# A two-layer encoder trunk on one core: four column blocks together in the FFN's first product, one block of x turned on TensorE, HBM reads issued later

## Chip, cores and metric

The kernel runs on one core of a Trainium2 chip. The metric is the device time of one execution in microseconds (us), the median of several executions of the same program.

## The reference

The reference is a pre-norm transformer encoder in 32-bit floats: 256 tokens of width D = 2048, two layers. The even layer mixes by retention and neighbourhood attention, the odd one by differential attention; each layer then has cross-attention into 256 memory tokens and a SwiGLU feed-forward network (FFN) with 5632 hidden columns. What stands around the change is this:

```python
def rms_norm(x, g):
    xf = x.astype(jnp.float32)
    y = xf * lax.rsqrt(jnp.mean(xf * xf, axis=-1, keepdims=True) + RMS_EPS)
    return (y * g.astype(jnp.float32)).astype(x.dtype)

def swiglu_ffn(h, w_in, w_out):
    g, u = jnp.split(h @ w_in, 2, axis=-1)
    return (jax.nn.silu(g) * u) @ w_out

# in each layer i, after the mixer:
    m = rms_norm(mem, norm_mem_g[i])
    x = x + memory_cross_attention(rms_norm(x, norm_xattn_g[i]), m, w_xq[i], w_xkv[i], w_xo[i], xq_g[i], xk_g[i])
    x = x + swiglu_ffn(rms_norm(x, norm_ffn_g[i]), w_ffn_in[i], w_ffn_out[i])
```

## The kernel before

**Layout.** x stays in SBUF as `x_sb`, the 256 tokens as two halves of 128 on the partitions, the 2048 columns as four blocks of 512. A product needs its left operand with the columns on the partitions, so x has to be turned before each of them. A product's left operand is kept as a pair of fp32r tiles, a rounded high part and a low part (`hTfh` and `hTfl` for the FFN, `hTxh` and `hTxl` for the cross-attention, `hTh` and `hTl` for the next layer's mixer), and so is each weight (`wh`, `wl`). Every product is the sum of three: high by `wh` (L313), high by `wl` (L314), low by `wh` (L315).

**Weights.** A weight piece of 512 rows by 512 columns (1 MB) is read by the SP queue into `raw`. `prepare()` makes from each half of it `wh` by a copy on ScalarE (L287) and `wl` by a subtraction on VectorE (L288), up to three units ahead of their use (`LOOK`). A *unit* is one such half, 256 rows by 512 columns: two row tiles, two token halves and three products make 12 matmuls of 128x512. `gemm()` runs the units of one weight matrix; the lists in `plan` set their order. By default a column block takes all its units before the next block begins. `woven(n, nu, early)` lets the first two column blocks take their first units, then the rest, then the blocks that are left: with 8 units, block 0 takes units 0 to 5, block 1 units 0 to 5, then 6 and 7 of each. Each column block holds two accumulators (`acc`, one per token half) in PSUM, out of a pool with two buffers of each.

**The FFN.** It runs in three groups of 4, 4 and 3 hidden blocks. In the first product (`w_ffn_in`) a hidden block is two column blocks, gate and up. All units with rows 0 to 511 need the left operand made of block 0 of x, those with rows 512 to 1023 need block 1, and so on.

**Turning x.** In the product before (`w_xo`, a single row piece, so two units to a block) the epilogue adds a finished block to x on VectorE (L722) and starts a *feed* of it. `regroup()` transposes 32x32 squares on VectorE into `zz` (L381, one instruction per token half), writes `zz` to a DRAM buffer `zd` on the SP queue (L383) and reads it back with the squares regrouped by four DMAs of the POOL queue (L385). The rest of the feed multiplies by the gain: ScalarE writes the high part (L400, four instructions), VectorE the low part (L402, eight). SP's queue also issues the weight reads, in its order.

**What sets the order.** Feeds and the attention's steps are generators held by a `Side` object. `gemm` takes one step of them after each unit (two where `steps=2`); a step waits for the count of units that the generator yielded, `MOVE = 5` between a feed's reads and its gain. A `gate` drains a feed before the unit that needs it. A scheduler then orders the instructions of each engine, so the queues are shown below as they stand in the built program.

## Time and profile before

| | before |
|---|---|
| three executions | 2489.2, 2491.04, 2495.09 us |
| median | 2491.04 us |
| profiled execution | 2492.25 us |
| its span, first to last instruction | 2490.3 us |
| granted TensorE clock, mean over the span | 0.998 |
| busy: TensorE / its weight loads / VectorE / ScalarE / GpSimd | 99 / 82 / 59 / 48 / 6 % |
| read from HBM | 487.93 MB, with the writes 206 GB/s over the span |

The span is measured on the profiled execution, and 1.95 us of that execution lie outside it. PE is TensorE, PEld its weight loads, DVE VectorE, ACT ScalarE, POOL GpSimd, SPq the queue of DMA issues on SyncE. In a row of a timeline stand the start in us, the duration, the engine, the line, the operation, what is written and from what, the shapes and the count; a bracket gives the engine's idle time just before and what ended it. "acc<-wh,hTfh" is a matmul into acc out of these two operands, hTfh the stationary one and wh the moving one with its 512 columns; "x8" is eight instructions told as one row.

### The profile page before, as it was taken

To read this page: it belongs to the slowest core of one execution; us is meant where nothing else is said; L and a number is where in the kernel's file an instruction comes from. 1 tells how busy PE (TensorE), PEld (TensorE's weight loads), DVE (VectorE), ACT (ScalarE), POOL (GpSimd) and SP (SyncE) were. 2 spreads that over 40 slices of the span, in tenths; PEclk is the share of its full clock that TensorE was granted. 3 is DMA by queue.
4 is the path that set the end of the run, shared out by engine and by line. 5 is a ranking of instruction groups with operands and counts; after the bars stand their busy time and mean duration, and the time that the engine had idled before them with its cause. 6 is when DMAs were issued, how large, how long until landed. Compare 5 with 4: busy or idle time off the path is not lost.

```text
span 2490.3 us, 28635 instructions
## 1 busy us (share of the span) xinstructions
PE 2459.9 (99%) x11168; PEld 2038.3 (82%) x11168; DVE 1480.4 (59%) x1845; ACT 1188.5 (48%) x1538; POOL 144.4 (6%) x223
## 2 busy tenths in 40 slices
PE   8999999999999999999999999999999999999999
PEld 6888888878888888888878888888788888888887
DVE  6775565775555555545567766766655545555554
ACT  5554464555443444444455555655544444443443
POOL 1000001110000000000010000010100000000000
PEclk9999999999999999999999999999999999999999
DMA  8545567566675666656675544674766556665665
GB/s 288 180 163 182 181 229 237 202 218 205 204 234 187 214 208 218 204 190 233 223 233 169 169 169 164 214 251 166 236 223 217 203 200 205 230 209 192 213 213 175
DMA packets 250856, 513.92 MB, mean 206 GB/s; under 512 B 11488, under 2 KB 12128, under 8 KB 250720
## 3 DMA queue, kind: packets, MB, share of 16 engines
q1 hardware_dynamic: 239856, 485.52, 57.1%
q0 software_dynamic: 8704, 24.13, 4.2%
q10 hardware_dynamic: 2160, 2.44, 0.3%
q8 instruction: 87, 1.43, 0.2%
q14 instruction: 49, 0.40, 0.0%
HBM read 487.93 MB, written 24.12 MB: 206 GB/s over the span
## 4 chain that ended last, share of the span: by engine, by line
PE 94%; DMA 3%; DVE 2%; issue 0%; ACT 0%; POOL 0%; ACTq 0%; POOLq 0%; DVEq 0%
PE acc L313 30%; PE acc L314 30%; PE acc L315 30%; DMA zd<-zz 1%; DMA zz<-zd 1%; PE pt L337 1%; DVE wl L288 1%; DMA raw<-in_w_in_ab 1%; DVE x_sb L722 0%; PE pt L526 0%; PE pa_s L418 0%; PE pa_s L417 0%; PE pa_s L416 0%; PE pa_r L576 0%; DVE zz L381 0%
## 5 line engine op out<-in xcount | busy, mean ns | idle before, releaser
L288 DVE TENSOR_TENSOR wl<-raw,wh 128x1024 fp32r<-128x1024 f32 (+1 forms) x865 | 1054.4, 1221 | 881.6 <-ACT wh L287 881.3
L287 ACT CAST wh<-raw 128x1024 fp32r<-128x1024 f32 (+1 forms) x865 | 909.6, 1052 | 1177.8 <-PE acc L315 1153.1
L313 PE MATMUL acc<-wh,hTfh 128*128 128x512 f32 x1408 | 550.8, 391 | 11.8 <-ACT hTfh L400 11.8
L314 PE MATMUL acc<-wl,hTfh 128*128 128x512 f32 x1408 | 549.7, 390 | 0.0
L315 PE MATMUL acc<-wh,hTfl 128*128 128x512 f32 x1408 | 548.6, 390 | 0.0
L313 PE MATMUL acc<-wh,hTh 128*128 128x512 f32 x832 | 331.8, 399 | 9.6 <-ACT wh L287 8.1
L314 PE MATMUL acc<-wl,hTh 128*128 128x512 f32 x832 | 325.6, 391 | 0.9 <-DVE wl L288 0.9
L315 PE MATMUL acc<-wh,hTl 128*128 128x512 f32 x832 | 325.5, 391 | 0.0
L313 PEld LDWEIGHTS acc<-wh,hTfh 128*128 128x128 f32 x1408 | 265.4, 189 | 69.2 <-ACT hTfh L400 14.3
L315 PEld LDWEIGHTS acc<-wh,hTfl 128*128 128x128 f32 x1408 | 265.4, 189 | 56.1 <-DVE hTfl L402 0.7
L314 PEld LDWEIGHTS acc<-wl,hTfh 128*128 128x128 f32 x1408 | 265.6, 189 | 55.1
L314 PE MATMUL acc<-wl,aTh 128*128 128x512 f32 x704 | 274.0, 389 | 2.9 <-DVE wl L288 2.9
L315 PE MATMUL acc<-wh,aTl 128*128 128x512 f32 x704 | 273.9, 389 | 0.0
L313 PE MATMUL acc<-wh,aTh 128*128 128x512 f32 x704 | 273.9, 389 | 0.0
L313 PEld LDWEIGHTS acc<-wh,hTh 128*128 128x128 f32 x832 | 156.9, 189 | 39.8 <-ACT wh L287 8.1
L315 PEld LDWEIGHTS acc<-wh,hTl 128*128 128x128 f32 x832 | 156.6, 188 | 33.9
L314 PEld LDWEIGHTS acc<-wl,hTh 128*128 128x128 f32 x832 | 157.0, 189 | 31.7 <-DVE wl L288 2.3
L385 POOL DMA_DIRECT2D zz<-zd x168 | 91.7, 553 | 1553.7 <-DMA zd<-zz 1450.3
L314 PEld LDWEIGHTS acc<-wl,aTh 128*128 128x128 f32 x704 | 132.1, 188 | 30.7 <-DVE wl L288 3.4
L313 PEld LDWEIGHTS acc<-wh,aTh 128*128 128x128 f32 x704 | 132.1, 188 | 27.5
L315 PEld LDWEIGHTS acc<-wh,aTl 128*128 128x128 f32 x704 | 132.1, 188 | 27.4
L313 PE MATMUL acc<-wh,oTh 128*128 128x512 f32 x256 | 100.2, 392 | 0.0
(185 smaller groups left out, 1939.7 us busy)
## 6 DMA issues: line engine op xcount, KB each, us to landing
raw<-in_w_ffn_in SPq DMA_DIRECT2D x176, 1024.0 KB, 4.9
raw<-in_w_ffn_out SPq DMA_DIRECT2D x88, 1024.0 KB, 5.1
raw<-in_w_in_ab SPq DMA_DIRECT2D x55, 1024.0 KB, 5.1
raw<-in_w_in_c SPq DMA_DIRECT2D x48, 1024.0 KB, 5.1
zd<-zz SPq DMA_DIRECT2D x42, 512.0 KB, 3.7
zz<-zd POOLq DMA_DIRECT2D x168, 128.0 KB, 4.9
raw<-in_w_out_ab SPq DMA_DIRECT2D x16, 1024.0 KB, 5.1
raw<-in_w_xkv SPq DMA_DIRECT2D x16, 1024.0 KB, 5.0
```

The lines of the kernel that those rows point to most:

```text
L287: nc.scalar.copy(wh[:, js], raw[:, rs])
L288: nc.vector.tensor_sub(wl[:, js], raw[:, rs], wh[:, js])
L313: nc.tensor.matmul(acc[t], lhsT=hi[:, kt, ts], rhs=wh[:, j], start=first and j == 0, stop=False)
L314: nc.tensor.matmul(acc[t], lhsT=hi[:, kt, ts], rhs=wl[:, j], start=False, stop=False)
L315: nc.tensor.matmul(acc[t], lhsT=lo[:, kt, ts], rhs=wh[:, j], start=False, stop=last and j == 1)
L337: nc.tensor.transpose(pt[:, j, t * P:(t + 1) * P], srcs[t][:, c:c + P], ident)
L385: nc.gpsimd.dma_start(zT[32 * j:32 * j + 32].rearrange("a (i n) -> a i n", i=4), zd[:, :, j].rearrange("i a n -> a i n"))
```

## The change

Three things change in the code.

- **Order of the first FFN product.** In the first group, `by_rows(n, 4)` takes the place of `woven(n, 8, 6)`: the first four column blocks take rows 0 to 511 together (two units each), then rows 512 to 1023, and so on; the other four follow one by one. Four blocks need eight accumulators. The third pair takes buffers of the pool `ps_t` and the fourth of `ps_a` (`wide`), which the attention uses at other times.
- **Block 0 of x turned on TensorE.** Between `w_xo` and the FFN, block 0 no longer goes through DRAM: `feed_turns`, as two tasks of one half each, turns it with TensorE transposes into PSUM (`turn`, four to a task) and writes the gain's high and low parts from there (`gained`). Blocks 1 to 3 go as before.
- **Reads issued later.** `regroup` becomes a generator with a step of `LAND = 2` units between the SP write and the four POOL reads, and one of `MOVE - LAND` after them. The sums of squares of a feed come ahead of it. This holds for all feeds and for the turning of the FFN's activations (`act_T`).

```diff
--- before.py
+++ after.py
@@ -24,7 +24,7 @@
 SCALE = HD ** -0.5
 LAM_INIT = 0.8 - 0.6 * math.exp(-0.3 * 1)
 NEG = -1e30
-MOVE = 5
+LAND, MOVE = 2, 5
 FFN_GROUPS = ((0, 4), (4, 8), (8, 11))
 
 OPENING = {2: (2, 3), 4: (-1,), 6: (4, 5), 8: (-2,), 10: (6, 7), 12: (-3,), 14: (-4,)}
@@ -226,6 +226,11 @@
         head += [(b, u) for b in range(lead) for u in range(early, nu)]
         return head + [(b, u) for b in range(lead, nblocks) for u in range(nu)]
 
+    def by_rows(nblocks, lead):
+
+        head = [(b, 2 * c + u) for c in range(4) for b in range(lead) for u in range(2)]
+        return head + [(b, u) for b in range(lead, nblocks) for u in range(8)]
+
 
     plan = []
 
@@ -254,7 +259,7 @@
         for g0, g1 in FFN_GROUPS:
             n = 2 * (g1 - g0)
             cols = [c + b * NB for b in range(g0, g1) for c in (0, HID)]
-            phase(w_ffn_in[layer], K4, cols, woven(n, 8, 6) if g0 == 0 else None)
+            phase(w_ffn_in[layer], K4, cols, by_rows(n, 4) if g0 == 0 else None)
             phase(w_ffn_out[layer], tuple(b * NB for b in range(g0, g1)), four, woven(4, n, n - 2))
     units = [(i, b, u) for i, ph in enumerate(plan) for b, u in ph[3]]
     ahead = deque()
@@ -289,7 +294,7 @@
         ahead.append((wh, wl))
         at["unit"] += 1
 
-    def gemm(kts, src, epi, gate=None, steps=1):
+    def gemm(kts, src, epi, gate=None, steps=1, wide=False):
         hi, lo = src
         w2, rows, cols, order = plan[at["phase"]]
         at["phase"] += 1
@@ -298,7 +303,10 @@
         for b, u in order:
             side.drain((gate or {}).get(u, ()))
             if b not in accs:
-                accs[b] = [ps_acc.tile([P, NB], F32, tag=f"acc{t}", name=f"acc{t}") for t in range(2)]
+                pools = ((ps_acc, f"acc{t}") for t in range(2))
+                if wide and b in (2, 3):
+                    pools = ((ps_t, "pt"), (ps_t, "pt")) if b == 2 else ((ps_a, "pa"), (ps_a, "pa"))
+                accs[b] = [q.tile([P, NB], F32, tag=tag, name=f"acc{t}") for t, (q, tag) in enumerate(pools)]
                 left[b] = nu
             while len(ahead) <= LOOK and at["unit"] < len(units):
                 prepare()
@@ -381,18 +389,29 @@
             nc.vector.transpose(zt[:, :, :, t], srcs[t].rearrange("p (k j a) -> p j k a", j=4, a=32))
         zd = dram.tile([4, 32, 4, T], F32, name="zd")
         nc.sync.dma_start(zd.rearrange("i a j n -> (i a) (j n)"), zt.rearrange("p j k t b -> p (j k t b)"))
+        yield LAND
         for j in range(4):
             nc.gpsimd.dma_start(zT[32 * j:32 * j + 32].rearrange("a (i n) -> a i n", i=4),
                                 zd[:, :, j].rearrange("i a n -> a i n"))
+        yield MOVE - LAND
         return zT.rearrange("p (i k t b) -> p i k t b", i=4, k=4, t=2)
 
+    def feed_turns(dst, b, u, srcs, gi, layer, ssr):
+
+        pt = turn(srcs, u)
+        for j in range(2):
+            k = 4 * b + 2 * u + j
+            gained(dst, k, pt[:, j], gain(gi, layer, k))
+        square_sum(ssr[0][:, u, b:b + 1], srcs[u])
+        return
+        yield
+
     def feed(dst, b, srcs, gi, layer, ssr, room):
-        zT = regroup(srcs, room)
         for t in range(2):
             square_sum(ssr[0][:, t, b:b + 1], srcs[t])
         if b == 3:
             finish_rstd(ssr)
-        yield MOVE
+        zT = yield from regroup(srcs, room)
         for k in range(4):
             g = gain(gi, layer, 4 * b + k)
             hi, lo = (x[:, 4 * b + k].rearrange("p (t i b) -> p t i b", t=2, i=4) for x in dst)
@@ -800,14 +819,16 @@
 
         def epi_xo(b, acc):
             add_x(acc, b)
-            tasks.extend(feed_x(hT, b, 3, layer, ssr, ("", "", "qT", "kT")[b]))
+            if b == 0:
+                tasks.extend(side.add(feed_turns(hT, b, u, x_block(b), 3, layer, ssr), u) for u in range(2))
+            else:
+                tasks.extend(feed_x(hT, b, 3, layer, ssr, ("", "", "qT", "kT")[b]))
 
         gemm((0,), xo, epi_xo, gate={0: heads[:2], 1: heads[2:]}, steps=2)
         gate = by_unit(tasks)
 
         def act_T(aT, zs, kt):
-            zT = regroup(zs)
-            yield MOVE
+            zT = yield from regroup(zs)
             for t in range(2):
                 split(*(x[:, kt:kt + 4, t * P:(t + 1) * P].rearrange("p k (i b) -> p k i b", i=4) for x in aT),
                       zT[:, :, :, t].rearrange("p i k b -> p k i b"))
@@ -830,7 +851,7 @@
                                                    in1=sgs[blk][t], op0=ALU.mult, op1=ALU.mult)
                 atasks.append(side.add(act_T(aT, sgs[blk], 4 * blk)))
 
-            gemm(KT4, hT, epi_in, gate=gate)
+            gemm(KT4, hT, epi_in, gate=gate, wide=g0 == 0)
             gate = None
             kts = tuple(4 * b for b in range(n))
             last = g1 == 11
```

**TensorE's queue in the `w_xo` product of layer 0**, where the first block is added to x and turned. `acc_4307` and `acc_4308` are the token halves of block 0, `acc_4343` and `acc_4344` those of block 1; `pt` is the transposes' PSUM tile. Before:

```order
L315 MATMUL acc_4307<-wh,xo 128x512
L315 MATMUL acc_4308<-wh,xo 128x512
L313 MATMUL acc_4308<-wh,xo 128x512
L314 MATMUL acc_4308<-wl,xo 128x512
L315 MATMUL acc_4308<-wh,xo 128x512
L315 MATMUL acc_4343<-wh,xo 128x512
L313 MATMUL acc_4343<-wh,xo 128x512
L314 MATMUL acc_4343<-wl,xo 128x512
L315 MATMUL acc_4343<-wh,xo 128x512
L313 MATMUL acc_4344<-wh,xo 128x512
```

And after:

```order
L323 MATMUL acc_4307<-wh,xo 128x512
L323 MATMUL acc_4308<-wh,xo 128x512
L321 MATMUL acc_4308<-wh,xo 128x512
L322 MATMUL acc_4308<-wl,xo 128x512
L323 MATMUL acc_4308<-wh,xo 128x512
L345 MATMUL pt<-ident,x_sb 128x128 x2
L323 MATMUL acc_4343<-wh,xo 128x512
L321 MATMUL acc_4343<-wh,xo 128x512
L322 MATMUL acc_4343<-wl,xo 128x512
L345 MATMUL pt<-ident,x_sb 128x128 x6
L323 MATMUL acc_4343<-wh,xo 128x512
L321 MATMUL acc_4344<-wh,xo 128x512
```

Eight transposes stand between the matmuls of block 1, two of them right after block 0's last matmul and six after three more; nothing of that kind stood there before.

**ScalarE's queue at the opening of the FFN in layer 0**: the copies that make `wh`, the sums of squares (`junk`), and the high parts of the FFN's left operand. Before:

```order
L287 CAST wh<-raw 128x1024 x2
L400 ACTIVATE hTfh<-zz,gcol 128x256 x4
L330 ACTIVATE junk,ssx<-x_sb 128x512 x2
L287 CAST wh<-raw 128x1024 x2
L400 ACTIVATE hTfh<-zz,gcol 128x256 x4
L287 CAST wh<-raw 128x1024
L400 ACTIVATE hTfh<-zz,gcol 128x256 x4
L287 CAST wh<-raw 128x1024 x3
L400 ACTIVATE hTfh<-zz,gcol 128x256 x4
L287 CAST wh<-raw 128x1024 x7
L826 ACT_TABLE_LOAD
```

And after, from the last sums of squares on (block 0's four stand a few rows ahead of this, read from `pt` on L350):

```order
L338 ACTIVATE junk,ssx<-x_sb 128x512 x2
L292 CAST wh<-raw 128x1024
L419 ACTIVATE hTfh<-zz,gcol 128x256 x4
L292 CAST wh<-raw 128x1024 x3
L419 ACTIVATE hTfh<-zz,gcol 128x256 x4
L292 CAST wh<-raw 128x1024 x2
L419 ACTIVATE hTfh<-zz,gcol 128x256 x4
L292 CAST wh<-raw 128x1024 x19
L847 ACT_TABLE_LOAD
```

Three feeds in place of four read `zz` here, with one, three, two and nineteen weight copies before, between and behind them.

**VectorE's queue at the end of layer 0**, in the last `w_ffn_out` product, where block after block of x is finished (`acc_9228` and `acc_9229` are block 2 before, `acc_9210` and `acc_9211` after) and fed to the next layer's `hT`. Before:

```order
L402 SCALAR_TENSOR_TENSOR hTl<-zz,gcol,hTh 128x128 x8
L288 TENSOR_TENSOR wl<-raw,wh 128x1024 x2
L402 SCALAR_TENSOR_TENSOR hTl<-zz,gcol,hTh 128x128 x8
L722 TENSOR_TENSOR x_sb<-acc_9228,x_sb 128x512
L722 TENSOR_TENSOR x_sb<-acc_9229,x_sb 128x512
L381 STREAM_TRANSPOSE zz<-x_sb 128x16x32 x2
L288 TENSOR_TENSOR wl<-raw,wh 128x1024 x6
```

And after:

```order
L421 SCALAR_TENSOR_TENSOR hTl<-zz,gcol,hTh 128x128 x8
L293 TENSOR_TENSOR wl<-raw,wh 128x1024 x2
L741 TENSOR_TENSOR x_sb<-acc_9210,x_sb 128x512
L741 TENSOR_TENSOR x_sb<-acc_9211,x_sb 128x512
L389 STREAM_TRANSPOSE zz<-x_sb 128x16x32 x2
L293 TENSOR_TENSOR wl<-raw,wh 128x1024
L421 SCALAR_TENSOR_TENSOR hTl<-zz,gcol,hTh 128x128 x8
L293 TENSOR_TENSOR wl<-raw,wh 128x1024 x5
```

The second group of eight `hTl` has moved behind the adds, the two square transposes and one `wl`.

## Rows read from the trace of the kernel before

**Rows 1.** Page, part 1: engine, busy us, share of the span, instructions.

```profile
PE 2459.9 (99%) x11168; PEld 2038.3 (82%) x11168; DVE 1480.4 (59%) x1845; ACT 1188.5 (48%) x1538; POOL 144.4 (6%) x223
```

**Rows 2.** TensorE's waits: us in total, times, longest.

```profile
PE acc L313 <- ACT hTfh L400: 11.8, 6, 2.6
...
PE acc L314 <- DVE wl L288: 3.9, 3, 2.9
```

**Rows 3.** Timeline of TensorE, end of layer 0 (start, duration, ..., [idle before, releaser]).

```profile
1263.41 0.50 PE L314 MATMUL acc<-wl,aTh 128*128 128x512 f32 x1 [2.94 <-DVE wl L288]
```

**Rows 4.** Timeline of TensorE, opening of the FFN in layer 0.

```profile
542.16 0.39 PE L315 MATMUL acc<-wh,xo 128*128 128x512 f32 x1
...
545.19 0.80 PE L313 MATMUL acc<-wh,hTfh 128*128 128x512 f32 x1 [2.64 <-ACT hTfh L400]
...
548.84 0.39 PE L313 MATMUL acc<-wh,hTfh 128*128 128x512 f32 x1
...
552.01 0.39 PE L315 MATMUL acc<-wh,hTfl 128*128 128x512 f32 x1
...
562.01 0.79 PE L313 MATMUL acc<-wh,hTfh 128*128 128x512 f32 x1 [2.11 <-ACT hTfh L400]
...
565.53 0.40 PE L315 MATMUL acc<-wh,hTfl 128*128 128x512 f32 x1
```

**Rows 5.** Timeline of TensorE, opening of the FFN in layer 1.

```profile
1759.64 0.39 PE L315 MATMUL acc<-wh,xo 128*128 128x512 f32 x1
...
1777.19 0.80 PE L313 MATMUL acc<-wh,hTfh 128*128 128x512 f32 x1 [2.38 <-ACT hTfh L400]
...
1780.70 0.39 PE L315 MATMUL acc<-wh,hTfl 128*128 128x512 f32 x1
```

**Rows 6.** Windows: stretch, length, busy PE PEld DVE ACT POOL, PEclk, DMA share, GB/s.

```profile
545.20:548.80 3.60, 3.60 (x9) 2.87 (x10) 3.23 (x10) 2.48 (x7) 0.00 (x0) 0.56 1.04 297
```

**Rows 7.** Timeline of ScalarE, the same opening and the end of layer 0.

```profile
544.63 1.71 ACT L400 ACTIVATE hTfh<-zz,gcol 128x256 fp32r<-128x256 f32 x4 [1.00 <-DMA zz<-zd]
...
561.45 1.71 ACT L400 ACTIVATE hTfh<-zz,gcol 128x256 fp32r<-128x256 f32 x4 [3.18 <-DMA zz<-zd]
563.06 1.03 ACT L287 CAST wh<-raw 128x1024 fp32r<-128x1024 f32 x1
...
1257.10 1.71 ACT L400 ACTIVATE hTh<-zz,gcol 128x256 fp32r<-128x256 f32 x4 [3.93 <-DMA zz<-zd]
```

**Rows 8.** Timeline of SP's queue, the `w_xo` product: writes of blocks 0 and 1.

```profile
531.79 0.34 SPq L383 DMA_DIRECT2D zd<-zz  x1
...
534.71 0.34 SPq L383 DMA_DIRECT2D zd<-zz  x1
```

**Rows 9.** Chain of waits: start and length of each link.

```profile
539.36 12.52 DMA zd<-zz
...
554.08 7.26 DMA zz<-zd
...
1240.55 6.23 DMA zd<-zz
```

**Rows 10.** Timeline of TensorE, eight transposes in the cross-attention of layer 0.

```profile
497.66 1.03 PE L337 MATMUL pt<-ident,z 128*128 128x128 f32 x8
...
498.45 0.48 PE L313 MATMUL acc<-wh,mTh 128*128 128x512 f32 x1
```

**Rows 11.** Timeline of VectorE, `w_xo` product and opening in layer 0.

```profile
528.53 0.69 DVE L722 TENSOR_TENSOR x_sb<-acc,x_sb 128x512 f32<-128x512 f32 x1 [1.02 <-PE acc L315]
...
561.99 2.19 DVE L402 SCALAR_TENSOR_TENSOR hTfl<-zz,gcol,hTfh 128x128 fp32r<-128x128 f32 x8 [2.46 <-ACT hTfh L400]
564.12 1.23 DVE L288 TENSOR_TENSOR wl<-raw,wh 128x1024 fp32r<-128x1024 f32 x1
```

**Rows 12.** Groups of VectorE by form: busy us, mean ns | idle before, releaser.

```profile
L381 DVE STREAM_TRANSPOSE zz<-x_sb 128x512 f32<-128x512 f32 x40 | 27.0, 694 | 0.1
...
L343 DVE SCALAR_TENSOR_TENSOR oTl<-pt,gcol,oTh 128x256 fp32r<-128x256 f32 x16 | 7.7, 481 | 2.5 <-ACT oTh L342 2.5
```

## The prediction

> **What bounds the kernel now.** I read four views in this order. The page's first part: TensorE is busy 99% of the span [rows 1], so only its idle time, its slow stretches and its own instructions can move the end. Second, TensorE's waits, five lines in all: the largest are 11.8 us for hTfh, in 6 waits, and 3.9 us for wl, 2.94 of it in one wait [rows 2, 3]; the rest belongs to the kernel's start, which the change leaves alone. Third, the matmuls where those six waits lie, the opening of the FFN in each layer. The full-speed step is (552.01 − 548.84) / 14 = 0.2264 us, so a unit of 12 matmuls takes 2.72 us. In layer 0 w_xo's last matmul starts at 542.16, w_ffn_in's first at 545.19, and full speed is back for good at 565.53 [rows 4], after 56 matmuls, which need 12.7 us: 565.53 − 542.39 − 12.7 = 10.4 us lost. In layer 1, 1780.70 − 1759.87 − 12.7 = 8.1 us [rows 5]. That exceeds the waits because the matmuls behind the longer ones ran at a granted clock of 0.56, the 1.2 GHz level for about eight of them [rows 6]: 8 × 0.2 = 1.7 us each time.
>
> Fourth, who is late. TensorE waits for hTfh, ScalarE's hTfh for the DMA zz<-zd [rows 7]: each 512-column block of x goes to DRAM and back to be turned. Block 0's hTfh starts at 544.63, 12.8 us after its write was issued at 531.79 [rows 7, 8]; block 2 needed 12.52 us for the write and landed at 561.34, a trip of 22.0 us [rows 9]. At the other place, the last FFN product of layer 0, the trip took 1257.1 − 1240.55 = 16.5 us; ScalarE stood 3.93 us at that hTh, the wh and wl behind it came late, and TensorE waited 2.94 us [rows 3, 7, 9].
>
> **The change, part by part.** *Row groups.* Four blocks take rows 0 to 511 together, so block 0 of x feeds 8 units, 21.8 us, where it fed 2 (5.4 us); blocks 1, 2, 3 are due 21.8, 43.5 and 65.3 us after the opening. No wait for hTf is left, and the openings give back 10.4 + 8.1 = **18.5 us**. Matmuls and weight reads keep their number. The second and third pair of accumulators sit in PSUM that no attention uses then: nothing.
>
> *x's block 0 on TensorE.* Per layer 8 transposes. Eight in a row stand between 497.66 and 498.45 [rows 10], 0.79 us; they come in two pieces, each with some 0.1 us until the step is regular again, say 1.1 us a layer with the exit, **−2.2 us**; bounds −1.6 and, if TensorE also stands for the adds, the third rival. The order puts the first two four matmuls' distance behind acc_4307's end, and VectorE starts the add there at once, after idling 1.02 us, for 0.69 us [rows 11]. So I count no wait. The Trainium skill (TensorE: Matmul & The Clock Gate, Part 4: PE-mode transpose) gives about 275 ns for one transpose inside a kernel. By that the sixteen would cost 4.4 us and the time would be some 2.4 us later; the row shows starts a tenth of a us apart, and the row decides.
>
> VectorE loses two zz transposes (0.694 each) and eight hTfl, and gains four hTfl of 256 columns (0.481 each) [rows 12]: 0.5 us more before block 1's write. ScalarE's four hTfh only move forward. One DRAM round trip of four falls away per layer.
>
> *Reads issued later.* The yield moves POOL's four issues in program order, behind one pow at most. POOL takes its reads when the write has landed, before and after: nothing by itself. But a feed now has three steps, and one is taken per unit, so in cross-attention block 3's x leaves five units earlier than ScalarE reads it (13.6 us), with two more units in hand: 19 us against the trips of 12.8 to 16.5. Cost nothing; with the 22.0 us trip it would be 3 us a layer. At the end of layer 0 the order also changes on VectorE: the adds, the zz and the wl that TensorE waited for stand ahead of the eight hTl. After the landing at 1257.1 come three of four hTh (1.3), wh (1.03), wl (1.23): 1260.7, needed at 1263.41 − 2.94 = 1260.47 [rows 3, 7, 11]. The write may leave one wl (1.23) later, and the next wl now stands behind the eight hTl (2.19) [rows 11]. I take back **+1.3 us** of the 2.94; bounds 0 and 2.9.
>
> *The wait it adds.* ScalarE takes its queue in order, and blocks 1 to 3 of hTfh now stand before the wh of units 4, 7 and 9 of the opening. If a landing is late, these wh, their wl and then TensorE are late. What follows a landing is four hTfh, wh, wl: from 561.45 to 564.12 + 1.23 = 565.35, about 4.0 us with the hand-over [rows 7, 11]. The opening starts at 542.39 + 1.1 = 543.5, unit 4 at 554.4, its first wl is used at 554.6: block 1 must land by 550.6. Its write was issued 2.9 us after block 0's, at 534.71 [rows 8]; with 1.1 us from TensorE and 0.5 from VectorE, 536.3. A trip of 12.8 us lands at 549.1, one of 16.5 at 552.8. Ahead of it is now one weight read, as block 0's had, so I take 14: 550.3, in time with nothing to spare. Blocks 2 and 3 leave some 4.7 us apart, as block 2 left after block 1 before (539.36 − 534.71) [rows 8, 9], and are due three and five units after block 1, 8.2 and 13.6 us: they gain room. For the margin I take 0.7 us a layer, **−1.4 us**; bounds 0 and the first rival.
>
> **Sum.** 18.5 − 2.2 + 1.3 − 1.4 = 16.2 us. The profiled execution took 2492.25 us, 1.95 of it outside its span, and would take 2476.0; the median of the three runs, 2491.04, lies 1.2 us lower: **2474.8 us**. I expect 2471 to 2478 for this case.
>
> **Rivals.** (1) *The wait moves to the weights.* Block 1 needs 16.5 us, as in the last FFN product. It lands at 552.8, 2.2 us late; waits of that length were followed by the half clock in both layers, 1.7 us more: 4.0 a layer, 8.0 in place of 1.4. 18.5 − 2.2 + 1.3 − 8.0 = 9.6: 2481.4. For it: the DMA share was 1.04 in the opening [rows 6], and without waits TensorE asks for weights sooner. Against: a quarter of the x traffic is gone. The Trainium skill (DMA: Bandwidth & Descriptors, Issuing engines are not separate DMA queues) says that transfers from all issuing engines run on the same 16 DMA engines and interleave; by that POOL's reads stay among the weights, the trace agrees with the share just named, and 2481.4 is what it would give.
>
> (2) *Slower.* The same place, with block 2's trip of 22.0 us for the first block: landing 558.3, 7.7 late, with the clock 9.4 a layer, 18.8 in all. 18.5 − 2.2 + 1.3 − 18.8 = −1.2: 2492.2. The gain is gone once a layer loses 8.8 us, at a trip of 21.4 us; slower by over 0.2% needs 24. Against it: 22.0 was the trip of a write with two weight reads and two x blocks ahead of it.
>
> (3) *The turn stalls TensorE.* The transposes stand in its queue behind matmuls and ahead of others. If both adds come a wl late, it stands 2 × (1.23 + 0.69) = 3.8 us a layer: 16.2 − 7.7 = 8.5, 2482.5. Against: VectorE was idle there [rows 11].
>
> (4) *It doesn't do what it says*: hTf's waits stay, since the gate drains late, only the costs remain: about 2492. The order shows hTfh from pt long ahead of the opening, so I give it little.
>
> **How the numbers follow.** Forecast 0.66, (1) 0.17, (3) 0.06, (2) 0.09, (4) 0.02. 0.2%, 5 us, is about what a measurement of this kernel can tell from no change. Forecast, (1) and (3) are faster by more: 0.89. (2) divides into 0.05 within 0.2% and 0.04 slower, (4) goes within: same 0.07. The range runs from 2470.5, with all of the boundary's 2.9 us gained and no late landing, to 2484, which holds (1) and (3); it leaves out some 0.15.
>
> **What would show it.** Right: TensorE's wait list has no hTfh line of several us; units of the opening at 2.72 us from 543.5 to 630 with the clock at 1.00; eight transposes from x_sb in w_xo's stretch with idle under 0.3 us; the wait for wl at the end of layer 0 about half. Wrong by (1) or (2): waits for wh or wl before units 4, 7, 9, with ScalarE standing at hTfh for zz<-zd. Wrong by (3): idle before a transpose, released by x_sb. Wrong altogether: new waits in cross-attention for hTxh or wh, where I count none, or at the end of the four-block head, where two act blocks leave for DRAM 10.9 us apart.

## The result and the profile after

The changed kernel took 2475.92 us (median of four runs, 2474.51 to 2477.23), the kernel before 2492.68 us in the four runs beside it: a ratio of 0.9941 (95% interval 0.9927 to 0.9955), faster by 0.6%. The forecast was 2474.8, with a range of 2471 to 2478. The profiled execution took 2475.84 us with a span of 2474.1, against 2490.3 before: 16.2 us less.

The first part of the page after, to set beside [rows 1], and TensorE's waits, to set beside [rows 2] (us in total, times, longest):

```profile
PE 2456.3 (99%) x11184; PEld 2037.1 (82%) x11184; DVE 1475.7 (60%) x1833; ACT 1187.0 (48%) x1538; POOL 138.2 (6%) x215
```

```profile
PE acc L321 <- ACT wh L292: 8.3, 1, 8.3
PE acc L322 <- DVE wl L293: 2.2, 6, 0.5
```

The line for hTfh, 11.8 us before, is gone. Of these two lines the first is the kernel's start (8.3), the second six waits for wl of half a us or less; the other two lines, 3.1 us together, stood before as well (2.5). TensorE's timeline in layer 0, from the last matmul of block 0 to the opening of the FFN, is to be set beside [rows 4]:

```profile
529.23 0.39 PE L323 MATMUL acc<-wh,xo 128*128 128x512 f32 x1
529.49 0.44 PE L345 MATMUL pt<-ident,x_sb 128*128 128x128 f32 x2
529.69 0.48 PE L323 MATMUL acc<-wh,xo 128*128 128x512 f32 x1
530.00 0.39 PE L321 MATMUL acc<-wh,xo 128*128 128x512 f32 x1
530.23 0.40 PE L322 MATMUL acc<-wl,xo 128*128 128x512 f32 x1
530.47 0.82 PE L345 MATMUL pt<-ident,x_sb 128*128 128x128 f32 x6
531.04 0.48 PE L323 MATMUL acc<-wh,xo 128*128 128x512 f32 x1
531.35 0.40 PE L321 MATMUL acc<-wh,xo 128*128 128x512 f32 x1
...
543.38 0.39 PE L323 MATMUL acc<-wh,xo 128*128 128x512 f32 x1
543.60 0.39 PE L321 MATMUL acc<-wh,hTfh 128*128 128x512 f32 x1
```

From 529.23 to 531.35 there are five steps from one matmul to the next, at 0.2265 us each 1.13 us; it took 2.12. The eight transposes cost 0.99 us. Then w_ffn_in's first matmul starts 0.22 us after w_xo's last one, where 2.64 us of waiting stood before. The window of the first four units (columns as in [rows 6]) has the clock at full:

```profile
543.60:554.50 10.90, 10.90 (x50) 9.03 (x49) 9.44 (x19) 7.16 (x12) 3.92 (x7) 1.00 0.96 304
```

**A ledger by stage** tells where the 16.2 us went. Each number is the difference between the starts of two first matmuls in TensorE's timeline; the stages are: w_xo and the first FFN product together, for each layer (first matmul of w_xo to first of w_ffn_out); the last w_ffn_out product of layer 0; the mixer's first product in layer 1; the query product of layer 1's cross-attention. At the regular step the first two would take 23.77 + 174.08 = 197.85 us (w_xo before, and 64 units of 2.72), and 198.84 with the transposes. The experiments stand in the same table, and so does one more profiled execution of each of the two kernels. The medians are of each row's own runs (before again had one). The sets of runs of before that were taken with the later rows have medians of 2488.1 to 2489.3, so a median is best compared through its ratio to its own set, and the stages with each other.

| kernel | w_xo + first FFN product, layer 0 | the same, layer 1 | last product, layer 0 | mixer's first product, layer 1 | query product, layer 1 | span | median |
|---|---|---|---|---|---|---|---|
| before | 208.35 | 206.01 | 68.56 | 296.36 | 22.73 | 2490.3 | 2492.68 |
| before again | 205.81 | 205.11 | 66.82 | 296.41 | 22.73 | 2485.2 | 2487.13 |
| after | 199.42 | 199.50 | 65.85 | 297.17 | 23.52 | 2474.1 | 2475.92 |
| after again | 198.95 | 199.92 | 65.58 | 296.80 | 22.73 | 2473.2 | 2476.22 |
| 1 row groups alone | 202.56 | 200.51 | 66.46 | 296.38 | 22.74 | 2477.1 | 2480.38 |
| 2 transposes alone | 202.17 | 202.43 | 66.24 | 296.43 | 22.73 | 2478.7 | 2486.64 |
| 3 later reads alone | 209.08 | 206.78 | 65.50 | 296.39 | 22.74 | 2489.1 | 2490.22 |
| 4 all but later reads | 199.40 | 200.89 | 66.43 | 296.42 | 22.73 | 2475.0 | 2474.69 |
| 5 two blocks turned | 199.86 | 199.83 | 66.39 | 296.42 | 25.03 | 2477.1 | 2479.54 |
| 6 writes doubled | 200.26 | 201.51 | 66.91 | 296.41 | 23.36 | 2477.0 | 2478.89 |
| 7 as 5, eight reads more | 199.82 | 199.77 | 67.44 | 296.65 | 22.96 | 2475.2 | 2476.99 |
| 8 no later reads in cross-attention | 199.02 | 200.95 | 65.58 | 296.99 | 22.74 | 2473.5 | 2475.07 |
| 9 a hop more | 202.73 | 203.96 | 65.69 | 296.45 | 23.13 | 2480.5 | 2483.98 |

Between the first profiles of before and after: 8.93 and 6.51 us gained in the two openings, 2.71 at the end of layer 0, 0.81 and 0.79 lost in the two stages of layer 1, and 0.35 lost at the start and the end: 16.2. The three places outside the openings have these rows in TensorE's timeline (before had 2.94 at the first, [rows 3], and no wait at the others):

```profile
1254.76 0.50 PE L322 MATMUL acc<-wl,aTh 128*128 128x512 f32 x1 [0.24 <-DVE wl L293]
...
1269.13 0.50 PE L322 MATMUL acc<-wl,hTh 128*128 128x512 f32 x1 [0.48 <-DVE wl L293]
...
1682.72 0.50 PE L322 MATMUL acc<-wl,hTxh 128*128 128x512 f32 x1 [0.49 <-DVE wl L293]
```

### The profile page after: what moved, and what is told of

Read it like the earlier page. It is cut to its first block, busy times and chain, and to the rows that moved or that the text cites. A ratio compares the mean times of both kernels' runs of the same rounds, so it can differ in the third digit from the quotient of the medians.

```text
span 2474.1 us, 28641 instructions
## 1 busy us (share of the span) xinstructions
PE 2456.3 (99%) x11184; PEld 2037.1 (82%) x11184; DVE 1475.7 (60%) x1833; ACT 1187.0 (48%) x1538; POOL 138.2 (6%) x215
## 4 chain that ended last, share of the span: by engine, by line
PE 92%; DMA 3%; DVE 3%; ACT 1%; POOL 1%; issue 0%; ACTq 0%; SPq 0%; POOLq 0%; DVEq 0%
PE acc L322 30%; PE acc L321 30%; PE acc L323 30%; DMA zz<-zd 2%; DVE wl L293 1%; DMA zd<-zz 1%; PE pt L345 1%; ACT wh L292 0%; PE pt L545 0%; PE pa_s L437 0%; PE pa_s L436 0%; DVE x_sb L741 0%; PE pa_s L435 0%; POOL zz L394 0%; PE pa_r L595 0%
```

## The experiments

**1. Row groups alone.** Block 0 goes through DRAM; regroup and feed are those of before.

```diff
-        yield LAND
...
-        yield MOVE - LAND
...
+        zT = regroup(srcs, room)
...
-        zT = yield from regroup(srcs, room)
+        yield MOVE
...
-            if b == 0:
-                tasks.extend(side.add(feed_turns(hT, b, u, x_block(b), 3, layer, ssr), u) for u in range(2))
-            else:
-                tasks.extend(feed_x(hT, b, 3, layer, ssr, ("", "", "qT", "kT")[b]))
+            tasks.extend(feed_x(hT, b, 3, layer, ssr, ("", "", "qT", "kT")[b]))
...
```

> Row groups alone: block 0 of x goes through DRAM as before, and the reads are issued with the write as before. My theory: the gain sits in the row groups. Of the six waits for hTfh only block 0's stays in each layer (2.64 and 1.54 us before, the longer with about 1.7 us of half clock behind it), blocks 1 to 3 are hidden. The openings give back 18.5 less 4.3 and 1.8, about 12.4 us; no transposes, the boundary at the end of layer 0 keeps its 2.94 us wait. Span about 2478, 12 us under the kernel before. Rival: it is the transposes that remove the trip which all others wait behind, and the row groups only move the waits to wh and wl in units 4 to 9: a gain of 5 us or less, with waits of 2 us or more for wh or wl in the opening.

Measured: 2480.38 us, the kernel before 2488.92 (25 runs), ratio 0.9971 (0.9961 to 0.998). The profiled span is 2477.1. TensorE's waits at the openings and at the end of layer 0, in this kernel's timeline:

```profile
545.60 0.80 PE L321 MATMUL acc<-wh,hTfh 128*128 128x512 f32 x1 [2.85 <-ACT hTfh L418]
...
1255.78 0.50 PE L322 MATMUL acc<-wl,aTh 128*128 128x512 f32 x1 [0.89 <-DVE wl L293]
...
1754.69 0.50 PE L321 MATMUL acc<-wh,hTfh 128*128 128x512 f32 x1 [2.34 <-ACT hTfh L418]
```

As the theory has it, only block 0's wait is left in each layer: 202.56 − 197.85 = 4.7 and 200.51 − 197.85 = 2.7 us lost, against 4.3 and 1.8 expected. No wait for wh or wl came in its place in the openings, so the rival falls. The row groups are the larger part of the gain: 8.5 us under 2488.92, where all but the later reads (experiment 4) gives 14.2.

**2. Block 0 on TensorE alone**, with `woven(n, 8, 6)` and the reads issued with the write.

```diff
-            phase(w_ffn_in[layer], K4, cols, by_rows(n, 4) if g0 == 0 else None)
+            phase(w_ffn_in[layer], K4, cols, woven(n, 8, 6) if g0 == 0 else None)
...
-        yield LAND
...
-        yield MOVE - LAND
...
-            gemm(KT4, hT, epi_in, gate=gate, wide=g0 == 0)
+            gemm(KT4, hT, epi_in, gate=gate, wide=False)
```

> Block 0 on TensorE alone: the old order of units (six of column block 0, six of column block 1) and the reads issued with the write. My theory: block 0's wait goes, but block 1 is due two units after it (5.4 us) and block 2 four (10.9 us), so their waits stay: in layer 0 block 2 lands near 559.2 and is due near 554.4, some 5 us of wait with 1.7 us of half clock. Of the 10.4 and 8.1 us that the openings lost 6 to 8 each remain, the transposes cost 1.0 a layer: a gain of 1 to 4 us, span about 2487. Rival: with block 0 out of the queue the other trips shorten so much that the old order is good enough: a gain of 10 us or more.

Measured: 2486.64 us, ratio 0.9992 (0.9983 to 1.0001): no difference that can be told. Its eleven runs lie from 2480.51 to 2490.5, and the profiled one is the shortest of them. In that one the waits in layer 0, for hTfh of blocks 1 and 2 and for a wh that stands behind one of them, are short:

```profile
549.85 0.50 PE L321 MATMUL acc<-wh,hTfh 128*128 128x512 f32 x1 [0.43 <-ACT hTfh L418]
...
556.70 0.73 PE L321 MATMUL acc<-wh,hTfh 128*128 128x512 f32 x2 [1.13 <-ACT wh L292]
...
558.29 0.50 PE L321 MATMUL acc<-wh,hTfh 128*128 128x512 f32 x1 [0.85 <-ACT hTfh L418]
```

The median is 2.3 us under 2488.92, and the interval, from 0.2 us slower to 4.2 faster, leaves room for the theory's 1 to 4 us and none for the rival's 10; by the profile alone, 11.6 us, one would have believed the rival. The place of the waits is as expected, blocks 1 and 2; the whole time varies by 10 us between executions of this one program. How much of the usual loss lies at which block can't be read from this one trace.

**3. The later reads alone**, the third part of the change put into the kernel before.

```diff
...
+        yield LAND
         for j in range(4):
             nc.gpsimd.dma_start(zT[32 * j:32 * j + 32].rearrange("a (i n) -> a i n", i=4),
                                 zd[:, :, j].rearrange("i a n -> a i n"))
+        yield MOVE - LAND
...
```

> The later reads alone, in the kernel before. My theory from the two traces: the wait for wl at the end of layer 0 falls from 2.94 to 0.2 us and the last product of layer 0 ends 2.7 us sooner; the next layer's first product loses 0.8 us and the second layer's cross-attention 0.8 us; the six waits for hTfh stay. Together 1.1 us less, span about 2489. Rival: what moved at these three places comes from the other two parts by way of the queues (the traffic of block 0 is gone from them): then all three places stay as in the kernel before.

Measured: 2490.22 us, ratio 1.0002 (0.9992 to 1.0011). The span came out as expected, 2489.1, and not for the reasons given: the last product of layer 0 is 3.06 us shorter than in the first profile of before, but neither of the two losses in layer 1 is there (296.39 and 22.74), and the openings lose 0.73 and 0.77 us more. My theory of the three places fell with it. Experiment 4 and the repeats of both kernels take them up again.

**4. All but the later reads.** The changed kernel with regroup and feed of before.

```diff
-        yield LAND
         for j in range(4):
             nc.gpsimd.dma_start(zT[32 * j:32 * j + 32].rearrange("a (i n) -> a i n", i=4),
                                 zd[:, :, j].rearrange("i a n -> a i n"))
-        yield MOVE - LAND
...
```

> The changed kernel with the reads issued with the write again. My theory: the wait for wl at the end of layer 0 is back at 2 to 3 us, the 0.5 us waits for wl at the start of layer 1 and in the second cross-attention are gone, the opening of the FFN stays free of waits over 0.6 us: span 2475 to 2476, 1 us over the changed kernel. Rival: the later reads are what keeps the traffic out of the openings, and their waits for wl grow to 2 us or more: span 2480 or over.

Measured: 2474.69 us, ratio 0.9949 (0.9936 to 0.9961), which can't be told from the whole change. No wait for wl in layer 1's two stages, and 0.84 us, not 2 to 3, at the end of layer 0. Layer 1's opening lost 1.4 us more than in the changed kernel, in waits of 0.62 and 0.76 us for wh and wl: no sign of the rival's 2 us.

**Repeats of both kernels.** Experiment 1 had 0.89 us at the end of layer 0 where the kernel before had 2.94, and there the two kernels have the same instructions in the same order on all engines.

> The changed kernel once more. In the two runs without the later reads (the third and the fourth) and in the first two, the waits for wl near 1255, 1269 and 1683 us came and went, and the first of them was 0.89 us in a kernel whose instructions stand there in the same order on every engine as in the kernel before, which had 2.94. My theory now: these three are the scatter of DMA trips from one execution to the next; they will have other sizes here (any of them between 0 and 1.5 us), while the openings again lose no more than 2.5 us a layer, transposes included, against 24 us for the w_xo product without them. Span 2471 to 2476. Rival: the three belong to the order of the later reads and come back within 0.1 us of 0.24, 0.48 and 0.49.

> The kernel before once more. My theory: waits for hTfh at the openings again, 8 to 13 us of loss in each layer's w_xo and first FFN product together with the clock, but the wait for wl at the end of layer 0 is another one than 2.94 us, between 0 and 2. Rival: 2.94 comes again within 0.2 us, and the 1.3 us that I counted for the boundary were owed to the order.

Measured: after again 2476.22 us, ratio 0.995 (0.9937 to 0.9964), with no wait over 0.1 us left at any of the three places (the mixer's product is still 0.4 us over its 296.4). Before again, 2487.13 in its one run; its timeline of TensorE, the opening and the end of layer 0:

```profile
546.51 0.50 PE L313 MATMUL acc<-wh,hTfh 128*128 128x512 f32 x1 [3.96 <-ACT hTfh L400]
...
1259.17 0.50 PE L314 MATMUL acc<-wl,aTh 128*128 128x512 f32 x1 [1.23 <-DVE wl L288]
```

The wait at the end of layer 0 was 1.23 us in this execution of the same program. So 2.94 was one draw of a size that varies from execution to execution. In the table the last product of layer 0 took 65.50 to 67.44 us in the eight profiles with later reads there (the two of the changed kernel, and 3 and 5 to 9), and 66.24 to 68.56 in the five without: they overlap, and the 2.71 us can't be put down to the change. The mixer's first product in layer 1 is another case: it took 296.36 to 296.43 us in the five without later reads, and 296.65 to 297.17 in four of the eight with them (7, 8 and both of the changed kernel). These losses, up to 0.8 us, came only with the later reads; no experiment tests how.

**5. Two blocks on TensorE.**

```diff
-            if b == 0:
+            if b <= 1:
                 tasks.extend(side.add(feed_turns(hT, b, u, x_block(b), 3, layer, ssr), u) for u in range(2))
```

> The changed kernel with block 1 of x turned on TensorE too: 16 transposes a layer in place of 8, and two DRAM trips in place of three. My theory: the second eight cost what the first eight did, 1.0 us a layer, and nothing of it is hidden; the wait behind block 2's late landing (0.3 us and as much of slow matmuls) goes, since its write has one trip less ahead. Together plus 0.8 us: span 2473.5 to 2476. Rival: TensorE stands at the transposes for the adds on VectorE, which now has four more pieces there: waits with x_sb as releaser of 1 us or more, up to 3.8 us a layer, span 2478 to 2482.

Measured: 2479.54 us (2478.89 to 2481.7), 3.3 to 3.6 over the changed kernel, and more than my theory had. The openings did what it said: w_xo took 25.78 us in layer 0 in place of 24.77, 1.01 us for the second eight transposes, with no wait for x_sb, so the rival falls; and the FFN product ran its 174.08 without any wait. Most of the extra time was elsewhere, in the query product of layer 1, 25.03 us, where nothing in the order differs from the changed kernel. TensorE's wait there, and POOL's queue that issues the reads of the block that came late:

```profile
1685.06 0.50 PE L322 MATMUL acc<-wl,hTxh 128*128 128x512 f32 x1 [1.66 <-DVE wl L293]
```

```profile
1639.30 2.17 POOL L394 DMA_DIRECT2D zz<-zd  x4 [15.84 <-DMA zd<-zz]
1666.51 1.09 POOL L394 DMA_DIRECT2D zz<-zd  x2 [25.04 <-DMA zd<-zz]
1669.82 1.10 POOL L394 DMA_DIRECT2D zz<-zd  x2 [2.21 <-issue]
```

Between the second and the third read of this block the queue stood for 2.21 us, with nothing in the profile that it waited for. Such a pause is in the traces of the kernels before and after and of experiments 1 to 4 as well, once in each, always after 8 reads of the bias and 98 of zz. With four reads fewer a layer, the 106th is another block's.

**6. Each write doubled.** Before the real write, the same zz is written to a buffer that nothing reads, in the FFN's feeds alone.

```diff
...
+        if twice:
+            ze = dram.tile([4, 32, 4, T], F32, name="ze")
+            nc.sync.dma_start(ze.rearrange("i a j n -> (i a) (j n)"), zt.rearrange("p j k t b -> p (j k t b)"))
...
-        zT = yield from regroup(srcs, room)
+        zT = yield from regroup(srcs, room, gi == 3)
```

> The changed kernel with each DRAM write of the FFN's feeds made twice, the first to a buffer that nothing reads: every trip of blocks 1 to 3 is 3 to 6 us longer, and TensorE's own work is the same. My theory: a landing later than its due time reaches TensorE one for one, through ScalarE's queue, in which the next wh stand behind hTfh: block 1 lands 551 to 553 in place of 548.3 and is due at 550.6, a wait of 0.5 to 2.5 us; block 2 lands near 565 and is due between 556 and 559, a wait of 6 us or more, with 1.7 us of half clock. Each layer loses 7 to 11 us, the span is 2488 to 2496, and the waits are for wh or wl, none for hTfh. Rival: the three units of wh and wl made ahead, and row groups that need a block only every 21.8 us, take up such a delay: a loss under 2 us a layer, span under 2478.

Measured: 2478.89 us, ratio 0.996 (0.9944 to 0.9975), span 2477.0. The trip did not lengthen as I had assumed. SP's writes and ScalarE's first reads of blocks 1 and 2 in layer 0:

```profile
536.63 0.43 SPq L394 DMA_DIRECT2D zd<-zz  x1
...
541.26 0.43 SPq L394 DMA_DIRECT2D zd<-zz  x1
```

```profile
551.54 1.71 ACT L422 ACTIVATE hTfh<-zz,gcol 128x256 fp32r<-128x256 f32 x4 [1.38 <-DMA zz<-zd]
...
558.40 1.71 ACT L422 ACTIVATE hTfh<-zz,gcol 128x256 fp32r<-128x256 f32 x4 [2.80 <-DMA zz<-zd]
```

Block 1 needed 14.9 us, 3.0 more than in the changed kernel, block 2 17.1, 1.1 less, and neither made TensorE wait. The scheduler also put block 1's hTfh one unit later. By the bounds stated the span is the rival's, under 2478, but with trips so little longer that decides nothing; experiment 9 lengthens them. Block 3 alone came late. Its first read by ScalarE in layer 0, and TensorE's wait 3.97 us later:

```profile
565.45 1.71 ACT L422 ACTIVATE hTfh<-zz,gcol 128x256 fp32r<-128x256 f32 x4 [3.45 <-DMA zz<-zd]
```

```profile
569.42 0.50 PE L322 MATMUL acc<-wl,hTfh 128*128 128x512 f32 x1 [0.76 <-DVE wl L293]
```

In layer 1 it was the same block, 3.95 us, and 2.06 us of waits for wh and wl.

**7. Two blocks on TensorE, and eight small reads more** on POOL's queue at the start, to move the count of its DMAs and nothing else.

```diff
+    spare = const.tile([P, 8], F32, name="spare")
+    for i in range(8):
+        nc.gpsimd.dma_start(spare[:, i:i + 1], gains[:, i:i + 1])
...
-            if b == 0:
+            if b <= 1:
```

> The fifth experiment's kernel (two blocks turned on TensorE) with eight small reads of 512 bytes added to POOL's queue at the kernel's start, of which nothing depends. In all nine traces so far POOL's queue stands still once, for 2.21 us with no releaser, right after its 106th DMA (8 bias reads and 98 reads zz<-zd). With two blocks a layer on TensorE the 106th falls into the middle of the four reads of the second cross-attention's last block, at 1668 us, and TensorE waits 1.66 us for wl at 1685. My theory: the pause goes by the count. With eight more ahead it moves to the reads of an earlier block (the 90th zz read), the wait at 1685 falls to 0 to 0.5 us as in the changed kernel, and the time falls by 1 to 2.5 us against 2479.5, to 2477 to 2478.5. Rival: the late landing at 1685 is traffic or the place of the buffers: the pause moves or not, the wait stays over 1.2 us and the time within 0.7 us of 2479.5.

Measured: 2476.99 us (2475.96 to 2477.13), 2.55 under experiment 5, span 2475.2. POOL's queue:

```profile
1618.38 1.09 POOL L394 DMA_DIRECT2D zz<-zd  x2 [3.81 <-PE acc L323]
1621.68 1.10 POOL L394 DMA_DIRECT2D zz<-zd  x2 [2.21 <-issue]
...
1667.09 2.18 POOL L394 DMA_DIRECT2D zz<-zd  x4 [24.44 <-DMA zd<-zz]
```

The same pause of 2.21 us now stands eight reads earlier, the block that was late is read in one piece, and the wait at 1685 is gone (the query product took 22.96). So the pause goes by what POOL's queue has issued before (though not by the plain count, as experiment 9 shows), and most of experiment 5's extra time came from where the smaller number had moved it. The median leaves two turned blocks about 1 us behind one, as the transposes' price would have it, but the runs of the two kernels overlap (2475.96 to 2477.13, and 2474.51 to 2479.59), so that this 1 us is not shown.

**8. No later reads in the cross-attention.**

```diff
...
-        yield LAND
+        if land:
+            yield land
...
-        yield MOVE - LAND
+        yield MOVE - land
...
-        zT = yield from regroup(srcs, room)
+        zT = yield from regroup(srcs, room, 0 if gi == 1 else LAND)
```

> The changed kernel, with the later reads everywhere but in the feeds of the cross-attention, which issue them with the write again. My theory: there the later reads only delay the last block's write, by some 6 us at the second cross-attention (it stood 9.9 us behind the start of the product with the memory's operand, and 3.4 in the kernel without them); the margin of that trip is then 6 us larger and no wait for wl is left in the products with hTxh. At the end of layer 0 the wait for wl is as in the runs with later reads, 0 to 0.8 us. Span 2471.5 to 2474, the time 0 to 1.5 us under the changed kernel. Rival: the waits of 0.3 to 1.7 us there are the scatter of the trips alone: one of 0.3 us or more shows here too.

Measured: 2475.07 us, ratio 0.9947 (0.9934 to 0.9959), span 2473.5. The query product of layer 1 took 22.74 us with no wait. In the seven profiles with later reads in the cross-attention it took 22.73, 22.74, 22.96, 23.13, 23.36, 23.52 and 25.03, in the six without always 22.73 or 22.74. The write of the block that comes late there, on SP's queue, in the changed kernel and then in experiment 4 (the product with the memory's operand begins at 1651.93 and 1652.33):

```profile
1661.81 0.34 SPq L391 DMA_DIRECT2D zd<-zz  x1
```

```profile
1655.69 0.34 SPq L391 DMA_DIRECT2D zd<-zz  x1
```

It is issued 9.9 us into the product with later reads and 3.4 without. But the margin is not 6 us larger without them, as I had expected, since ScalarE's read moves along with the write. Its first read of that block, in the changed kernel and then in experiment 4:

```profile
1674.36 0.91 ACT L419 ACTIVATE hTxh<-zz,gcol 128x256 fp32r<-128x256 f32 x2 [1.24 <-DMA zz<-zd]
```

```profile
1667.09 1.70 ACT L418 ACTIVATE hTxh<-zz,gcol 128x256 fp32r<-128x256 f32 x4
```

ScalarE is free for it 1674.36 − 1.24 − 1661.81 = 11.3 us behind the write with later reads, and 1667.09 − 1655.69 = 11.4 us without. What differs is the trip. The last read landed 10.5 to 11.2 us behind the write in the six profiles without later reads there, so ScalarE never waited. In the seven with them it landed 10.4 to 14.0 us behind it: ScalarE waited in five (0.67, 0.85, 1.04, 1.24 and, with POOL's pause in the trip, 2.76 us), and each time the product lost some 0.45 us less than that. So the small losses there come with the later reads: 0 to 0.8 us by how long the trip happens to be, and 2.3 with the pause. Why the trip is longer at the later time is not shown. The gain in the median, about 1 us, is within the intervals; this version and experiment 4 are the changed kernel's equals, not shown to be better.

**9. A hop more.** In the FFN's feeds of blocks 1 to 3 the block is written to a second buffer first and copied from there, in series.

```diff
...
+        ze = dram.tile([4, 32, 4, T], F32, name="ze") if hop else zd
-        nc.sync.dma_start(zd.rearrange("i a j n -> (i a) (j n)"), zt.rearrange("p j k t b -> p (j k t b)"))
+        nc.sync.dma_start(ze.rearrange("i a j n -> (i a) (j n)"), zt.rearrange("p j k t b -> p (j k t b)"))
+        if hop:
+            nc.gpsimd.dma_start(zd.rearrange("i a j n -> (i a) (j n)"), ze.rearrange("i a j n -> (i a) (j n)"))
         yield LAND
...
-        zT = yield from regroup(srcs, room)
+        zT = yield from regroup(srcs, room, gi == 3)
```

> The changed kernel with one more hop through DRAM, in series, in the FFN's feeds of blocks 1 to 3 (the block is written to a second buffer, copied from it to the first by POOL's queue, then read back), so that each trip is some 6 to 12 us longer. The scheduler puts the high parts of block 1 before the wh of unit 5 in place of 4, of block 2 before unit 9 in place of 7, of block 3 before 11 in place of 9. My theory: a landing reaches TensorE one for one through ScalarE's queue: where a landing is late, the first wl behind it is used 3.96 us, give or take 0.1, after the first hTfh of that block starts, as it was in both layers of the changed kernel (3.96 and 3.97). Block 1 is due at 543.6 + 5 x 2.72 + 0.23 - 3.96 = 553.5 and lands near 558 to 560, so TensorE waits 4 to 7 us in units 5 or 6; both layers together lose 8 to 16 us, span 2482 to 2490, and no wait is for hTfh. Rival: the row groups' 21.8 us of margin take up the delay: no wait over 2 us, span under 2478.

Measured: 2483.98 us (2480.34 to 2487.52), ratio 0.9981 (0.9972 to 0.999); the profiled span, 2480.5, is among the shortest. ScalarE's first read of block 1 in the two layers, and then TensorE's waits behind it:

```profile
557.16 1.70 ACT L422 ACTIVATE hTfh<-zz,gcol 128x256 fp32r<-128x256 f32 x4 [6.89 <-DMA zz<-zd]
...
1766.25 1.71 ACT L422 ACTIVATE hTfh<-zz,gcol 128x256 fp32r<-128x256 f32 x4 [6.51 <-DMA zz<-zd]
```

```profile
559.85 0.50 PE L321 MATMUL acc<-wh,hTfh 128*128 128x512 f32 x1 [2.51 <-ACT wh L292]
561.11 0.50 PE L322 MATMUL acc<-wl,hTfh 128*128 128x512 f32 x1 [0.76 <-DVE wl L293]
...
1768.94 0.50 PE L321 MATMUL acc<-wh,hTfh 128*128 128x512 f32 x1 [2.14 <-ACT wh L292]
1770.21 0.50 PE L322 MATMUL acc<-wl,hTfh 128*128 128x512 f32 x1 [0.76 <-DVE wl L293]
```

561.11 − 557.16 = 3.95 and 1770.21 − 1766.25 = 3.96 us, as expected. The sizes came out smaller: the waits are 3.3 and 2.9 us in place of 4 to 7, since the block landed a little sooner than I had put it, and the span is 1.5 us under the 2482 to 2490 expected. In layer 0 the block was due at 553.5 and came 3.7 us late; the first wl was used at 561.11 in place of 543.58 + 13.60 + 0.23 = 557.41, 3.7 us late, and the product took 177.94 in place of 174.08. The lateness reaches TensorE one for one, by way of wh and wl, and none of it as a wait for hTfh. In layer 1 the product lost 5.1 us, of which the two waits are 2.9; of the rest, 1.6 us are eight slow matmuls between 1771.0 and 1774.2, 0.2 us longer each, at the 1.2 GHz level (granted clock 0.50 from 1770.8 to 1774.2). The rival falls: the row groups give a block more time until it is used, but not more time until ScalarE stands in front of it. POOL's queue shows its pause here too, a little longer and after the first of four reads:

```profile
1639.87 0.55 POOL L397 DMA_DIRECT2D zz<-zd  x1 [19.04 <-DMA zd<-zz]
1642.79 1.64 POOL L397 DMA_DIRECT2D zz<-zd  x3 [2.36 <-issue]
```

## Why the prediction was right, point by point

**What bounded the kernel** was read right: the six waits with the half clock behind them. The openings lost 10.5 and 8.2 us against the regular step (10.4 and 8.1 were forecast), and the changed kernel lost 0.58 and 0.66 over its transposes. The size of such a loss varies too: the second execution of before lost 7.96 and 7.26.

**Row groups: right.** Alone they leave exactly block 0's wait in each layer, and with the transposes no wait for hTfh is left.

**The transposes: right.** 0.99 us a layer against 1.1, and 1.01 for another eight. The Trainium skill (TensorE: Matmul & The Clock Gate, Part 4: PE-mode transpose) has about 275 ns for one inside a kernel, from which an estimate would be 2.2 us a layer. In these runs a transpose between matmuls costs 0.12 us, and the measurement decides. Row groups and transposes belong together: alone the transposes gain nothing that can be told, since in the old order blocks 1 and 2 are due two and four units after block 0.

**The wait it adds: mechanism right, block wrong.** I had the danger at block 1, due at 550.6, with a trip of 14 us. ScalarE and SP's queue after the change:

```profile
548.35 1.71 ACT L419 ACTIVATE hTfh<-zz,gcol 128x256 fp32r<-128x256 f32 x4 [0.77 <-DMA zz<-zd]
...
559.34 1.71 ACT L419 ACTIVATE hTfh<-zz,gcol 128x256 fp32r<-128x256 f32 x4 [3.60 <-DMA zz<-zd]
```

```profile
536.41 0.34 SPq L391 DMA_DIRECT2D zd<-zz  x1
...
541.06 0.34 SPq L391 DMA_DIRECT2D zd<-zz  x1
```

Block 1's write left at 536.41 (536.3 forecast) and needed 11.9 us: in time by 2.3. Block 2 needed 18.3 us and came at 559.34, due at 558.8; TensorE's wait is this row, 3.96 us later:

```profile
563.30 0.50 PE L322 MATMUL acc<-wl,hTfh 128*128 128x512 f32 x1 [0.27 <-DVE wl L293]
```

"They gain room" is the step of the prediction that failed. Block 2 is due 8.2 us after block 1 and leaves 4.65 after it, 3.5 us of room, but its trip is 6.3 us longer; [rows 9] had shown 22.0 us for it, which I used for the second rival and not here. The amount was near all the same: 0.6 us a layer where I took 0.7, and 0.1 and 1.1 us in the second execution (198.95 and 199.92, less 198.84). So the nearness of 0.6 to 0.7 is partly luck: the wait sat at another block. It is the first rival's mechanism at about a seventh of its 4.0 us; experiment 9 shows it in full, 3.9 and 5.1 us a layer.

**The boundary, +1.3: not shown to be owed to the change.** I costed a wait of 2.94 us from one profiled execution as if it were the program's. The same program had 1.23 in another one, and the same order 0.89 in experiment 1. The profiles gave +2.71 (a wait of 0.24 where I had about half of 2.94 left), of which the change has at most a part.

**Cost nothing in the cross-attention: wrong, by 0.8 us in the first profile of the changed kernel and by nothing in the second.** I gave that trip 19 us from write to use. It has 11.2 to 11.4 us until ScalarE, in its order, stands in front of it, with later reads or without (experiment 8). In some executions the trip was longer than that, in others not.

**The sum** came out at 16.2 us, the forecast's 16.2, and that is luck: the openings gave 15.4 where the forecast had 14.9, the boundary 1.4 more than forecast, and against these 1.9 us stand two losses of 0.8 in layer 1 and 0.35 at the start and the end. It was also made against an execution at the upper end of the kernel before: the 25, 11 and 15 runs beside the experiments have medians of 2488.92, 2488.11 and 2489.3, by which the change is worth some 12 to 13 us, 0.5%. The openings, 15.4 of the 16.2, are the part whose cause the experiments show. Of the rivals, TensorE stood for no add, and neither (2) nor (4) is in any run of the changed kernel.

**Slips in the working** move nothing above. 8 × 0.2 is 1.6, where the rows give 1.6 and 1.7. All of the boundary's 2.9 us and no late landing make 2471.8 and not 2470.5. The accumulators in the attention's PSUM are the third and fourth pair. The 4.4 us estimated for sixteen transposes are 2.2 more than the 2.2 counted, not 2.4.

**What the three parts are worth.** Row groups and transposes together are the change: 2474.69 without the later reads, 2475.92 and 2476.22 with them. The later reads bring nothing that these runs can tell, alone (ratio 1.0002) or on top. None of these versions beats the changed kernel by more than the intervals.

## What to carry to other kernels

A wait on a DMA trip in one profile is one draw: before an edit is credited with it, profile the same program twice, and compare the stages between two fixed instructions rather than the spans. When a product is short of its operand at the start, let several output blocks share each slice of the operand, and make the first slice without the trip; here each alone left waits that the other removes. A margin has to be counted to the place where the reading engine's queue meets the data, with what stands behind it there, and not to where the data is used; and a change that moves the write may move that place with it.

## What the runs showed of the hardware

- **POOL's queue pauses once, by what it has issued.** In both profiles of before, both of after and those of experiments 1 to 8, it stood 2.21 or 2.22 us after its 106th DMA issue. Eight unrelated issues at the start moved the pause by eight reads. In experiment 9 a pause of 2.36 us comes after the 108th issue: 8 reads of the bias, 97 of zz and 3 of the copies, which have another shape. So the plain count is not the rule, and what is counted stays open. Four reads fewer a layer shifted it into a trip without slack; with it moved away again the median was 2.55 us lower.
- **The clock after a wait does not go by the wait's length.** Waits of 2.64 us at the same place were followed by a granted clock of 0.56 in the kernel before [rows 6], part of that stretch at the 1.2 GHz level, and by 1.00, the 2.4 GHz level, in experiment 3, in this window:

```profile
545.46:549.10 3.64, 3.64 (x16) 3.00 (x17) 3.01 (x11) 3.06 (x8) 0.00 (x0) 1.00 1.04 326
```

In the kernel before, 2.94 us of waiting [rows 3] were followed by 1.00 too (window 1263.4 to 1267.0), and 2.11 us [rows 4] by 0.52 (562.02 to 565.6).

- **Where trips are exposed, the time scatters.** The runs of before spread over 10 us (2484.43 to 2494.67 in the set of 11), those of the transposes alone as much; the changed kernel's ten spread over 5, experiment 4's five over 4 (2473.03 to 2476.81). The wait for one trip of the same program was 2.94 us in one execution and 1.23 in another.
